# A half chunk of gate and up taken into the turns of the second seven-product chunk, in a one-core decoder layer

## The chip, the cores and the metric

The kernel runs on one core of a Trainium2 chip. The metric is the device time in microseconds (us) of one execution. Before the change the median of three runs is 292.05 us (291.76 to 292.76).

## The reference, cut to what matters

One decoder layer over 256 tokens with a model width of 1024. The first half (attention heads and a convolution side by side, then an output projection) is not touched by the change. The second half is a SwiGLU feed-forward network with a hidden width of 2816:

```python
h = rms_norm(x, norm2_g[l])
x = x + (jax.nn.silu(h @ w_gate[l]) * (h @ w_up[l])) @ w_down[l]
```

All values are float32. The kernel gets that precision out of TensorE by splitting each operand into a rounded high part and the rest, and by three matmuls for each product (high by high, high by low, low by high).

## The kernel before, in words

Tokens lie in two row blocks of 128 (i = 0, 1). The 2816 gate and up columns are cut into chunks (`WIDTHS`): chunks 0 to 2 and 4, 5 with 512 columns of each, chunk 3 with 256 (the half chunk). Two ways of computing a chunk stand side by side:

- A plain chunk is computed as it is written. Its units are `("g", c, z, kh, a)`, or `("h", 3, 0, kh, a)` for the half chunk, where gate and up share one weight block. Each unit has four products (L892 to L904). The half chunk has four units, here h0 to h3, and two PSUM banks, `fg30` and `fg31`.
- A shared chunk (1, 4 and 5) uses a seven-product scheme in place of eight: units s0 to s6 (`shared_unit`, L906 to L921), each with four products. Its weights are sums of blocks. s1 and s2 need an addition on VectorE (L271) for each of their two pieces; each of these additions is followed by an accumulating DMA (L285), issued by GpSimd, that makes the sum which s4 or s6 will use. The partial products go to the banks U and V (tag "s", two banks) and, at s3, W (tag "t", two banks).

The down-projection follows as row units f0 to f21 (`row`, L925), four products each: for both row blocks and both halves of the output, one tile of 128 hidden rows. Its four accumulators `pd` take the four banks of tag "mm" when f0 begins, in the order `pd00`, `pd01`, `pd10`, `pd11`; the half chunk's `fg30` and `fg31` are the last two tenants of that tag before them.

Weights come in blocks of 1 MB by DMA from SyncE's queue, in the order in which they are used: four buffers of tag "raw", and three homes (`big_h`, `big_l`, `side`) for the blocks of the shared chunks that are used more than once. Half a block is a piece of 1024 columns. `feed` (L265) turns pieces into operands: the addition where there is one (VectorE), the rounded copy `wh` (ScalarE, L272), and the difference `wl` (VectorE, L277). A plain unit or a row unit takes one piece, a shared unit takes two. `feed` is called when a unit begins, and once more in the middle of a shared unit. At piece number `at` it puts out additions and copies up to piece at + 5 and differences up to piece at + 4. Seven buffers hold split pieces, so the copy of a piece waits until TensorE has finished the piece seven before it.

The work after a product (silu, products with the gate, transposes back) is put out by tasks. `step` (L226) runs after every second product, that is in the middle and at the end of each unit. When h3 is done, `gate2_task` (L817, two silu on ScalarE) runs at the end of the next unit; `up2_task` (L821) puts out the first of two `times` (L813, VectorE, which read `fg30` and `fg31`) in the middle of the unit after that, the second at its end, and then the transposes (`turned`, L801 to L809), half a unit apart: TensorE into a bank of tag "t", then a ScalarE copy (L807) and a VectorE difference (L809).

Each engine keeps the order in which instructions were written (`keep_order`, L175). Buffers and banks are given out by the framework, which adds the waits. An engine may run far ahead of the others within these waits. The order of the units is what `_order` (L70) returns.

Of the kernel before, what the change touches and what calls it, by code (L numbers as in the profile page):

```python
# [64 lines left out]
SHARED = (1, 4, 5)  # L65
HOMES = ("big_h", "big_l", "side")
FIRST_TURN = 3


def _order():  # L70

    chunk = lambda c: [("g", c, z, kh, a) for z in range(2) for kh in range(2) for a in range(2)]
    rows = lambda a, b: [("f", f) for f in range(a, b)]
    order = [("g", 0, z, kh, a) for kh in range(2) for z in range(2) for a in range(2)]

    def stage(c, others):
        for j in range(8):
            if j < 7:
                order.append(("s", c, j))
            order.append(others[j])  # L80

    stage(1, chunk(2))
    order.extend(("h", 3, 0, kh, a) for kh in range(2) for a in range(2))
    stage(4, rows(0, 8))
    stage(5, rows(8, 16))
    return order + rows(16, NF)


def _plan():
# [15 lines left out]
    for kind, *unit in _order():  # L105
        if kind != "s":
            i, a = (base + unit[0] // 2, unit[0] % 2) if kind == "f" else (block[tuple(unit[:3])], unit[3])
            if a == 0:
                loads.append(i)
            sources.append((i, a, None, (("load",),) if a else ()))  # L110
            continue
        c, j = unit
        n = SHARED.index(c)
        b11, b21, b12, b22 = quarters[n]
        after = (None,) * 4 if n + 1 == len(SHARED) else quarters[n + 1]
        i, add, more, then = ((b11, None, None, None), (b11, b12, (b12, b22), None), (b11, b22, (b11, b21), None),
                              (b21, None, None, "load"), (b12, None, None, after[0]), (b22, None, None, after[2]),
                              (b11, None, None, after[3]))[j]
        if i == b21:
            loads.append(i)  # L120
        for a in range(2):
            acts = (("add",) + more,) if more else ()
            if a and then is not None:
                acts += (("load",),) if then == "load" else (("home", then),)
            sources.append((i, a, add, acts))
# [67 lines left out]
def _build(nc, tc, t, ctx):  # L193
# [627 lines left out]
    def up2_task(c, banks, width):  # L821
        ups = []
        for i in range(NT):
            ups.append(times(c, i, banks[i][:, W - width:] if width < W else banks[i], ffn["s", c][i], width))
            yield 1
        yield 0 if c else FIRST_TURN
        for i in range(NT):
# [105 lines left out]
    for kind, *unit in _order():  # L933
        feed(at + LEAD)
        if kind in "gh":
            plain_unit(*unit)
        elif kind == "s":
            shared_unit(*unit)
            at += 1
        elif unit[0] < NF - LAST:  # L940
            for i in range(NT):
                for n in range(2):
                    row(unit[0], i, n, wpart(at, n))
        else:
            last[unit[0]] = at
        at += 1
# [66 lines left out]
```

## Time and profile before

| what | value |
|---|---|
| median of three runs | 292.05 us |
| the profiled execution's own time | 291.87 us |
| its span, first to last instruction | 290.1 us |
| TensorE (PE) busy | 282.8 us, 97% |
| VectorE (DVE) busy | 226.3 us, 78% |
| ScalarE (ACT) busy | 181.8 us, 63% |
| GpSimd (POOL) busy | 24.9 us, 9% |
| HBM read | 61.55 MB |

The profile is of one execution. PE is TensorE's matmuls, PEld its weight loads, SPq the queue of SyncE that issues DMAs. A row of a timeline gives start, duration, engine, line of the kernel, operation, output and inputs by the program's names (buffer numbers left out) with their shapes, how many instructions were merged, and in brackets the idle time before it and who ended it. The durations of neighbours on PE overlap; the distance between two starts is what a matmul costs there.

### The profile page before, as it was taken

Reading aid. Unit: us, or ns where it says so; the run is one execution under the profiler, and the core shown is the slowest. Engines: PE = TensorE matmul, PEld = TensorE weight load, DVE = VectorE, ACT = ScalarE, POOL = GpSimd, SP = SyncE. Lnnn points to the kernel's source line nnn. Section 1 sums busy time; section 2 is a strip of 40 time slices with the busy share of each in tenths; the row PEclk is TensorE's granted clock in tenths of the full one; section 3 lists DMA queues with packets and bytes.
Section 4 is the critical chain, followed back from the end, with each engine's and each line's share of the span. In section 5 each row is a group of like instructions: output and inputs, shape, how many; then the busy total and the mean of one; then the engine's idle time right before and its main releaser. Section 6 shows DMA issues by size and latency. Waiting matters only on the chain.

```text
span 290.1 us, 3686 instructions
## 1 busy us (share of the span) xinstructions
PE 282.8 (97%) x1321; PEld 229.8 (79%) x1321; DVE 226.3 (78%) x339; ACT 181.8 (63%) x271; POOL 24.9 (9%) x46
## 2 busy tenths in 40 slices
PE   8999999999999999999999999889999999999994
PEld 6888877678688888888888888678888888888883
DVE  3899995999972957999997759978779996787211
ACT  5776768989815778655987453667754487656000
POOL 0005372000000000010200001120001020000000
PEclk9999999999999999999999999999999999999999
DMA  7999878643704589359999961897795888300011
GB/s 252 415 414 353 351 245 300 236 145 137 297 4 145 184 311 375 139 172 225 189 370 375 337 224 19 157 242 252 298 359 158 165 204 323 129 16 2 0 72 74
DMA packets 12052, 62.84 MB, mean 217 GB/s; under 512 B 1601, under 2 KB 2209, under 8 KB 6274
## 3 DMA queue, kind: packets, MB, share of 16 engines
q1 hardware_dynamic: 9874, 54.86, 50.6%
q0 software_dynamic: 2016, 7.74, 14.0%
q8 instruction: 10, 0.16, 0.2%
q14 instruction: 8, 0.07, 0.1%
q10 hardware_dynamic: 144, 0.00, 0.0%
HBM read 61.55 MB, written 1.05 MB: 216 GB/s over the span
## 4 chain that ended last, share of the span: by engine, by line
PE 92%; DVE 3%; DMA 1%; issue 1%; ACT 1%; SPq 0%; ACTq 0%
PE pd L723 20%; PE p L684 18%; PE fg L723 17%; PE U L723 10%; PE po L723 8%; PE V L723 6%; PE W L723 3%; PE aT L804 2%; DMA Y<-dw_b 1%; PE warm L341 1%; PE S L527 1%; DVE wl L277 1%; PE pT L557 1%; DVE raw L271 1%; PE x2T L746 1%
## 5 line engine op out<-in xcount | busy, mean ns | idle before, releaser
L277 DVE TENSOR_TENSOR wl<-raw,wh 128x1024 fp32r<-128x1024 f32 x108 | 129.5, 1221 | 11.4 <-ACT wh L272 10.9
L272 ACT ACTIVATE wh<-raw 128x1024 fp32r<-128x1024 f32 x108 | 111.8, 1057 | 35.6 <-DVE raw L271 12.5
L723 PE MATMUL pd<-wh,act 128*128 128x512 f32 x176 | 57.4, 393 | 1.8 <-DVE ac L813 1.8
L723 PE MATMUL fg<-wh,g 128*128 128x512 f32 x160 | 52.1, 394 | 0.0
L723 PEld LDWEIGHTS pd<-wh,act 128*128 128x128 f32 x176 | 33.1, 188 | 8.9 <-issue 2.2
L723 PEld LDWEIGHTS fg<-wh,g 128*128 128x128 f32 x160 | 30.1, 188 | 6.1
L723 PE MATMUL pd<-wl,act 128*128 128x512 f32 x88 | 34.3, 390 | 0.0
L684 PE MATMUL p<-wh,xh 128*128 128x512 f32 x80 | 33.0, 412 | 0.0
L684 PE MATMUL p<-wh,xl 128*128 128x512 f32 x80 | 31.4, 392 | 0.0
L723 PE MATMUL fg<-wl,g 128*128 128x512 f32 x80 | 31.2, 390 | 0.0
L684 PE MATMUL p<-wl,xh 128*128 128x512 f32 x80 | 26.6, 394 | 0.0
L285 POOL DMA_DIRECT2D raw<-w x12 | 10.5, 876 | 179.5 <-DVE raw L271 118.4
L807 ACT ACTIVATE act<-aT 128x512 fp32r<-128x512 f32 (+1 forms) x12 | 6.6, 560 | 21.4 <-PE aT L804 21.4
L723 PEld LDWEIGHTS pd<-wl,act 128*128 128x128 f32 x88 | 16.6, 188 | 3.3
L684 PEld LDWEIGHTS p<-wh,xh 128*128 128x128 f32 x80 | 15.2, 190 | 3.7 <-issue 0.7
L684 PEld LDWEIGHTS p<-wh,xl 128*128 128x128 f32 x80 | 15.2, 189 | 3.1
L684 PEld LDWEIGHTS p<-wl,xh 128*128 128x128 f32 x80 | 15.2, 189 | 3.0
L723 PEld LDWEIGHTS fg<-wl,g 128*128 128x128 f32 x80 | 15.1, 188 | 2.9
L809 DVE TENSOR_TENSOR act<-aT,act 128x512 fp32r<-128x512 f32 (+1 forms) x12 | 7.7, 645 | 11.8 <-ACT act L807 11.8
L723 PE MATMUL U<-wh,g 128*128 128x512 f32 x48 | 16.1, 392 | 0.0
L271 DVE TENSOR_TENSOR raw<-raw,raw 128x1024 f32<-128x1024 f32 x12 | 14.6, 1218 | 0.0
L723 PE MATMUL po<-wh,mixh 128*128 128x512 f32 x32 | 12.6, 395 | 0.0
(179 smaller groups left out, 413.8 us busy)
## 6 DMA issues: line engine op xcount, KB each, us to landing
raw<-w SPq DMA_DIRECT2D x45, 1024.0 KB, 5.1
raw<-w POOLq DMA_DIRECT2D x12, 512.0 KB, 5.5
first<-first SPq DMA_DIRECT2D x8, 384.0 KB, 5.8
xtok<-xtok SPq DMA_DIRECT2D x2, 512.0 KB, 9.1
x<-xtok SPq DMA_DIRECT2D x2, 512.0 KB, 7.4
out<-o SPq DMA_DIRECT2D x4, 256.0 KB, 2.0
inv<-inv POOLq DMA_DIRECT2D x1, 768.0 KB, 7.5
fwd<-fwd POOLq DMA_DIRECT2D x1, 648.0 KB, 4.3
```

What stands on the lines that cost most here:

```text
L271: nc.vector.tensor_tensor(src, src, blocks[add][:, cut(a)], op=ALU.add)
L272: nc.scalar.activation(dst[0], src, AF.Copy)
L277: nc.vector.tensor_tensor(dst[1], src, dst[0].bitcast(F32), op=ALU.subtract)
L285: nc.gpsimd.dma_start(blocks[to][:, cut(a)], t["w"][more - 2][:, cut(a)], accum_op=ALU.add)
L341: nc.tensor.matmul(warm[:, 0:T], zeros[:, 0:P], zeros, start=True, stop=True)
L527: nc.tensor.matmul(banks[a][:, out], G["qT"][rows, j, q], G["kT"][rows, j, k], start=True, stop=True)
L557: nc.tensor.transpose(b[:, a * P:(a + 1) * P], p[:, a * P:(a + 1) * P], ident)
L684: nc.tensor.matmul(banks[i], (xh, xh, xl)[a][:, kt, sls[i]], w[a % 2], start=kt == 0 and a == 0, stop=kt == KT - 1 and a == 2 - (order[-1] ...
L723: nc.tensor.matmul(bank, l, r, start=start and a == 0, stop=stop and a == 2, skip_group_check=on)
L804: nc.tensor.transpose(b[:, a, :], u[:, a * P:(a + 1) * P], ident)
L807: nc.scalar.activation(hi, b[:, 0:nf, :], AF.Copy)
L809: nc.vector.tensor_tensor(lo, b[:, 0:nf, :], hi.bitcast(F32), op=ALU.subtract)
```

## The change

Before, the four units of the half chunk stand alone, and then the units of chunk 4 take turns with f0 to f7. After, the half chunk's units are the first partners of chunk 4, and the row units begin after s3. The list `MIXED` fixes the turns ("s" is the next shared unit, "p" the next of the others):

- before: h0 h1 h2 h3 | s0 f0 s1 f1 s2 f2 s3 f3 s4 f4 s5 f5 s6 f6 f7
- after: h0 s0 h1 h2 s1 h3 s2 s3 f0 f1 s4 f2 f3 s5 f4 s6 f5 f6 f7

Counted from h0's piece as piece 0, the pieces before are h0 to h3: 0 to 3, s0: 4 and 5, f0: 6, s1: 7 and 8, f1: 9, s2: 10 and 11, f2: 12, s3: 13 and 14, f3: 15, s4: 16 and 17. After, they are h0: 0, s0: 1 and 2, h1: 3, h2: 4, s1: 5 and 6, h3: 7, s2: 8 and 9, s3: 10 and 11, f0: 12, f1: 13, s4: 14 and 15, f2: 16, f3: 17, s5: 18 and 19. Stages 1 and 5 keep their turns. The number of instructions of every kind stays the same. The list of loads follows the same order, so the block of s3 is now loaded ahead of the blocks of f0 to f3.

```diff
+MIXED = "psppspssppsppspsppp"
...
-    def stage(c, others):
-        for j in range(8):
-            if j < 7:
-                order.append(("s", c, j))
-            order.append(others[j])
-
-    stage(1, chunk(2))
-    order.extend(("h", 3, 0, kh, a) for kh in range(2) for a in range(2))
-    stage(4, rows(0, 8))
-    stage(5, rows(8, 16))
+    def stage(c, others, turns):
+        others = iter(others)
+        j = iter(range(7))
+        for turn in turns:
+            order.append(("s", c, next(j)) if turn == "s" else next(others))
+
+    half = [("h", 3, 0, kh, a) for kh in range(2) for a in range(2)]
+    stage(1, chunk(2), "spspspspspspspp")
+    stage(4, half + rows(0, 8), MIXED)
+    stage(5, rows(8, 16), "spspspspspspspp")
```

## The prediction

> **What bounds the kernel now.** I read the page's busy times first, then the waits of TensorE (PE), then a table of stages around the change, then the timelines of each engine there.
>
> ```profile
> PE 282.8 (97%) x1321; PEld 229.8 (79%) x1321; DVE 226.3 (78%) x339; ACT 181.8 (63%) x271; POOL 24.9 (9%) x46
> ```
>
> PE is busy nearly throughout, so a reordering that leaves every matmul in place can gain only where PE stands still. The waits of PE, by line, with total, count and longest in us:
>
> ```profile
> PE pd L723 <- DVE ac L813: 1.8, 1, 1.8
> PE warm L341 <- DVE one L324: 1.0, 1, 1.0
> PE cv L296 <- DVE yl L254: 0.2, 1, 0.2
> ```
>
> The second is at the start and the third in the convolution. In the feed-forward part there is one wait: an accumulator `pd` of the down-projection waits for `ac`, the product on VectorE (DVE) that reads the half chunk's banks. The table of stages (window, length, then busy time of PE, weight loads, DVE, ACT, POOL, granted clock, DMA share) puts it in its surroundings:
>
> ```profile
> 171.00:183.40 12.40, 12.40 (x63) 10.23 (x62) 9.26 (x11) 5.07 (x7) 1.75 (x2) 1.00 0.41 108
> 183.40:189.40 6.00, 4.24 (x19) 3.20 (x18) 6.00 (x7) 3.96 (x7) 0.23 (x1) 1.00 0.80 178
> 189.40:202.20 12.80, 12.78 (x58) 10.58 (x59) 10.23 (x11) 8.73 (x11) 1.52 (x2) 1.00 0.87 228
> ```
>
> The first row is h0 to h3: PE is full, DVE has about 3 of 12.4 us free. The second is s0 and f0: DVE is full, PE is not. The clock is 1.00 in all three, so the only price is the stall itself. PE's timeline:
>
> ```profile
> 186.12 0.39 PE L723 MATMUL pd<-wh,act 128*128 128x512 f32 x1
> ...
> 187.02 0.39 PE L723 MATMUL pd<-wl,act 128*128 128x512 f32 x1
> 187.25 0.39 PE L723 MATMUL pd<-wh,act 128*128 128x512 f32 x1
> 189.42 0.47 PE L723 MATMUL pd<-wh,act 128*128 128x512 f32 x1 [1.78 <-DVE ac L813]
> ```
>
> Six matmuls of f0 (two accumulators) run from 186.12; the seventh, `pd10`, needs the bank of `fg30`. Matmuls start 0.23 us apart (187.02 to 187.25), so it was due at 187.48 and began at 189.42: 1.94 us are lost. DVE's rows tell why:
>
> ```profile
> 169.17 1.22 DVE L277 TENSOR_TENSOR wl<-raw,wh 128x1024 fp32r<-128x1024 f32 x1
> 173.71 0.69 DVE L809 TENSOR_TENSOR act<-aT,act 128x512 fp32r<-128x512 f32 x1 [3.32 <-ACT act L807]
> 174.31 0.74 DVE L813 SCALAR_TENSOR_TENSOR ac<-fg,rstd,sf 128x512 f32<-128x512 f32 x1
> 174.97 1.22 DVE L277 TENSOR_TENSOR wl<-raw,wh 128x1024 fp32r<-128x1024 f32 x1
> 176.11 0.74 DVE L813 SCALAR_TENSOR_TENSOR ac<-fg,rstd,sf 128x512 f32<-128x512 f32 x1
> 176.77 1.22 DVE L271 TENSOR_TENSOR raw<-raw,raw 128x1024 f32<-128x1024 f32 x1
> 177.90 1.22 DVE L277 TENSOR_TENSOR wl<-raw,wh 128x1024 fp32r<-128x1024 f32 x1
> ...
> 186.53 1.22 DVE L271 TENSOR_TENSOR raw<-raw,raw 128x1024 f32<-128x1024 f32 x1
> 187.66 1.22 DVE L277 TENSOR_TENSOR wl<-raw,wh 128x1024 fp32r<-128x1024 f32 x1
> 188.79 0.87 DVE L813 SCALAR_TENSOR_TENSOR ac<-fg,rstd,sf 128x256 f32<-128x256 f32 x2
> ```
>
> The four L271 additions of s1 and s2 (the first at 176.77, the last at 186.53) stand in DVE's queue right before the two half-width `ac`. Starts of neighbours give what each operation costs in a full queue: 1.14 us for an addition or a difference, 0.66 for a full-width `ac`, 0.60 for an L809. ScalarE's (ACT) rows:
>
> ```profile
> 167.23 0.68 ACT L798 ACTIVATE sg<-U,rstd 128x512 f32<-128x512 f32 x1
> 167.80 2.00 ACT L272 ACTIVATE wh<-raw 128x1024 fp32r<-128x1024 f32 x2
> ...
> 186.55 0.82 ACT L798 ACTIVATE sf<-fg,rstd 128x256 f32<-128x256 f32 x2
> 188.82 0.58 ACT L858 ACTIVATE s<-U 128x512 f32<-128x512 f32 x1
> ```
>
> The two silu were done at 187.37, so `ac` lacked nothing but its turn on DVE. A copy L272 costs ACT 0.95 to 1.06 us.
>
> **The change, part by part.** PE executes the same matmuls. One unit costs it
>
> ```profile
> 196.97 2.72 PE U L723 x12
> ```
>
> 2.72 us, plus the transposes that fall into it.
>
> *Where PE stands.* The first five units are h0 to h3 and s0 before, h0, s0, h1, h2, s1 after, with the same transposes in them. So h3 now begins at 186.12, s2 at 188.84, s3 at 191.56, f0 at 194.28, and `pd10` is due at 195.64.
>
> *What DVE does until then.* The order in which it is written, from the additions on (piece numbers of the section on the change): addition 5 stands ahead of the difference that began at 169.17, and both end by 171.5 in DVE's free stretch before 173.71. Then: L809 173.71, `ac` 174.31, addition 6 at 174.97, difference 5 at 176.11, `ac` 177.25, difference 6 at 177.91, addition 8 at 179.05, difference 7 at 180.19, two L809 from 181.33, addition 9 at 182.53, difference 8 at 183.67. The copy of piece 9 waits for addition 9 (183.75) and ends at 184.8. From there copies and differences follow each other at 1.14: differences 9 to 14 begin at 184.9, 186.0, 187.2, 188.3, 189.5, 190.6. Then comes the first half-width `ac` at 191.8 (0.44 us, half of the 0.87), difference 15 at 192.2, and the second `ac` at 193.4.
>
> *Against what PE needs.* Piece 9 is used in the middle of s2, at 190.2, and is ready at 186.1; pieces 10 and 11 (s3, 191.56 and 192.92) are ready at 187.2 and 188.4. `pd10` is due at 195.64 and its bank is free at 192.4 (the earlier stall ended 0.2 after its `ac`); `pd11` about 0.7 later, its bank free at 194.0. Smallest cushion in this list: some 2 us at `pd11`. One more sits earlier: the transposes of chunk 2's second row block, in the middle of the unit after s0, at about 178.6, need the `ac` that now ends at 178.0, a cushion of 0.4 us. So the stall goes: minus 1.94 us.
>
> *What is late next.* s3 now has W in one of the two banks of tag "t" while the half chunk's transposes come in f0. Those rows, from the timelines of the three engines before:
>
> ```profile
> 192.23 0.38 PE L804 MATMUL aT<-c_ident,ac 128*128 128x128 f32 x2
> 192.64 0.38 ACT L807 ACTIVATE act<-aT 128x256 fp32r<-128x256 f32 x1 [2.29 <-PE aT L804]
> 193.06 0.42 DVE L809 TENSOR_TENSOR act<-aT,act 128x256 fp32r<-128x256 f32 x1 [1.13 <-ACT act L807]
> 193.84 0.38 PE L804 MATMUL aT<-c_ident,ac 128*128 128x128 f32 x2
> ```
>
> The second pair starts 1.61 after the first; the first bank is free 1.25 after it (193.48), and some 0.2 for the signal. Before, another bank was free anyway; now W has it, so the second pair must wait for the first pair's bank (margin 0.2 us), or for W's, which is read by the next DVE operation:
>
> ```profile
> 205.16 0.69 DVE L863 TENSOR_TENSOR c<-W,s 128x512 f32<-128x512 f32 x1 [0.40 <-PE W L723]
> ```
>
> Bounds: nothing, if the first bank is given and ACT and DVE are free then (my table has ACT's queue empty by 194.5 and DVE's by 194.9); 0.4 if it is W's (0.36 for the L809 ahead of it, 0.69 for itself, less the margin); with one late copy ahead of L807, up to 1.5. I take 0.05, because that table leaves both engines a us. A gain here is excluded: no wait stood there.
>
> *DMAs and queues.* s1 and s2 are moved ahead of f0 to f2, and with them their four accumulating DMAs on GpSimd's queue:
>
> ```profile
> 178.60 0.88 POOL L285 DMA_DIRECT2D raw<-w  x1 [38.11 <-ACT act L807]
> 182.22 0.87 POOL L285 DMA_DIRECT2D raw<-w  x1 [2.75 <-DVE raw L271]
> DMA to landing us min/median/max: 5.3/5.5/6.8
> ```
>
> Those of s1 now go out after additions 5 and 6, at about 171 and 176.5, and land by 183.3 at the latest; the copies that read them (pieces 14 and 15) come at 189 and 191: 6 us of cover. GpSimd has nothing else queued. The blocks that the additions read come from SyncE's queue:
>
> ```profile
> 151.35 1.46 SPq L245 DMA_DIRECT2D raw<-w  x2
> 156.32 3.60 SPq L245 DMA_DIRECT2D raw<-w  x2
> DMA to landing us min/median/max: 4.7/6.0/8.4
> ```
>
> The block for s1's additions is the first of the pair at 151.35, the one for s2's the first at 156.32: landed by 159.8 and 164.7, needed at 169.2 and 179.0. Nothing. The loads for f0 to f7 go out later in the turn order, but each goes four blocks ahead of its use, over 20 us; DMA was used at 0.41 in the first stage. U's last reader is the silu at 167.23, before s0's new start at about 174. Nothing.
>
> [...] The 182.22 row stood in a stretch where DVE never paused, and took 0.87 as its neighbour did. [...]
>
> *Sum.* 291.87 − 1.94 + 0.05 = 290.0 for an execution like the profiled one, which lies 0.18 below the median of the runs shown; 292.05 − 1.89 = 290.2 by the median. I forecast **290.0**.
>
> **The rivals.**
>
> 1. *The stall goes (forecast), 289.5 to 290.4.* For: the waiting `ac` gets three more units, 8.2 us, between h3 and f0's need, of which the moved additions' backlog takes none. Chance 0.66.
> 2. *A shorter wait takes its place, at the second transposes of the half chunk:* 0.4 to 1.5 as above, so 290.4 to 291.5. For: two banks, three tenants within one unit. Against: the margin is positive by the rows. Chance 0.14, nearly all under 291.2.
> 3. *Nothing is gained, 291.5 to 292.5.* The additions and the neighbours s2 s3 (four pieces in 5.4 us) could push DVE's queue out so that `ac` is late again; DVE's 1.14 for a piece against PE's 1.36 speaks against it, but additions, L809 and `ac` come on top, and my table would have to be wrong by 3 us. Chance 0.11.
> 4. *Slower: the second accumulating DMA of s1 lands late.* ACT takes its queue in order: the copy of piece 15 would hold back that of piece 16, the copy L858, that of piece 17 and the L807 of the transposes in f0, and the second transposes hold PE. That chain is 3 × 1.0 + 0.58 + 0.38 + 0.42 + 0.2, about 4.6 us, so it decides if the landing is after 192.7. [...] Against: 9 us of margin over the worst landing of the rows. Chance 0.05. [...]
>
> Other mishaps (the 0.4 us cushion at 178.6, a load in the wrong order) get 0.04, slower.
>
> **How the numbers follow.** The range 289.5 to 291.4 takes the first case and nearly all of the second: 0.8. About 0.3% (0.9 us) is what a measurement of this kernel can tell from no change. Faster by more than that, under 291.2: 0.66 + 0.12 = 0.78. Within it: 0.02 + 0.11 = 0.13. Slower: 0.05 + 0.04 = 0.09.
>
> **What would show it right or wrong.** Right: the wait of `pd` for `ac` is gone from PE's waits; the first L271 of the stage starts near 169 in place of 176.77 and the fourth near 182.5; the half-width `ac` run near 192 and 193.5, before f0; f0 starts near 194.3 without a pause inside. Case 2: a PE wait at `aT` for L809 or L863 within f0. Case 3: the wait of `pd` remains, with L277 rows ahead of `ac`. Case 4: ACT idle before an L272 with a DMA as what ended it. The forecast is wrong if PE's busy time shrinks by less than the span, that is if new waits add up to over 1 us.

## The result, and the profile after

The changed kernel takes 289.98 us in the median (289.64 to 290.64), the kernel before beside it 292.18: a ratio of 0.9926, with a 95% interval of 0.9901 to 0.9952. The profiled execution of the changed kernel took 289.81 us, its span is 288.0 us (before 291.87 and 290.1). The lines after are one higher than before from `_order` on (L271 is now L272, L813 is L814).

First the waits of PE after, in the columns of the prediction (line and what it waited for, total, count, longest):

```profile
PE warm L342 <- DVE one L325: 1.0, 1, 1.0
PE cv L297 <- DVE yl L255: 0.2, 1, 0.2
```

The wait of `pd` for `ac` is gone and no other has come. The stage table after, for the same two windows:

```profile
171.00:183.40 12.40, 12.40 (x63) 10.23 (x61) 10.22 (x12) 5.70 (x8) 1.75 (x2) 1.00 0.72 157
183.40:189.40 6.00, 6.00 (x28) 4.98 (x27) 5.95 (x6) 5.55 (x7) 1.75 (x2) 1.00 0.72 209
```

VectorE (the third busy time) does 10.22 us in the first window, 1.0 more than before. In the second it is still full, 5.95 of 6.00, but PE is full too: what stands in its queue then is no longer needed at once. VectorE's timeline after:

```profile
169.18 1.22 DVE L272 TENSOR_TENSOR raw<-raw,raw 128x1024 f32<-128x1024 f32 x1
170.31 1.22 DVE L278 TENSOR_TENSOR wl<-raw,wh 128x1024 fp32r<-128x1024 f32 x1
...
182.54 1.22 DVE L272 TENSOR_TENSOR raw<-raw,raw 128x1024 f32<-128x1024 f32 x1
183.67 8.17 DVE L278 TENSOR_TENSOR wl<-raw,wh 128x1024 fp32r<-128x1024 f32 x7
191.76 0.48 DVE L814 SCALAR_TENSOR_TENSOR ac<-fg,rstd,sf 128x256 f32<-128x256 f32 x1
192.15 1.22 DVE L278 TENSOR_TENSOR wl<-raw,wh 128x1024 fp32r<-128x1024 f32 x1
193.28 0.48 DVE L814 SCALAR_TENSOR_TENSOR ac<-fg,rstd,sf 128x256 f32<-128x256 f32 x1
193.68 1.22 DVE L278 TENSOR_TENSOR wl<-raw,wh 128x1024 fp32r<-128x1024 f32 x1
196.48 0.42 DVE L810 TENSOR_TENSOR act<-aT,act 128x256 fp32r<-128x256 f32 x1 [1.58 <-ACT act L808]
196.82 0.68 DVE L864 TENSOR_TENSOR c<-W,s 128x512 f32<-128x512 f32 x1
```

The first addition fills the idle time that stood before 173.71, and the fourth runs at 182.54 (before at 186.53). Seven differences follow, and then the two half-width `ac`, before f0. PE's timeline there:

```profile
194.28 0.39 PE L724 MATMUL pd<-wh,act 128*128 128x512 f32 x1
...
195.41 0.39 PE L724 MATMUL pd<-wh,act 128*128 128x512 f32 x1
195.64 0.38 PE L805 MATMUL aT<-c_ident,ac 128*128 128x128 f32 x2
195.78 0.48 PE L724 MATMUL pd<-wh,act 128*128 128x512 f32 x1
...
197.02 0.39 PE L724 MATMUL pd<-wh,act 128*128 128x512 f32 x1
197.25 0.38 PE L805 MATMUL aT<-c_ident,ac 128*128 128x128 f32 x2
```

f0 runs through. The transposes at 195.64, the first to need the first half-width `ac`, come 3.4 us after its end (191.76 + 0.48), the seventh matmul (195.78) 3.5. The second transposes start at 197.25, before the end of L864 (197.50), so they did not get W's bank but that of the first transposes, which L810 left at 196.90.

### The profile page after: what moved, and what is told of

Read it like the earlier page. It is cut to its first block, busy times and chain, and to the rows that moved or that the text cites. A ratio compares the mean times of both kernels' runs of the same rounds, so it can differ in the third digit from the quotient of the medians.

```text
span 288.0 us, 3690 instructions
## 1 busy us (share of the span) xinstructions
PE 282.5 (98%) x1321; PEld 229.5 (80%) x1321; DVE 225.9 (78%) x339; ACT 181.3 (63%) x271; POOL 24.9 (9%) x46
## 4 chain that ended last, share of the span: by engine, by line
PE 95%; DVE 3%; issue 1%
PE pd L724 21%; PE fg L724 19%; PE p L685 18%; PE U L724 11%; PE po L724 8%; PE V L724 6%; PE W L724 3%; PE aT L805 2%; PE warm L342 1%; PE S L528 1%; PE pT L558 1%; PE x2T L747 1%; PE cv L297 1%; DVE wl L278 0%; PE cv L298 0%
## 5 line engine op out<-in xcount | busy, mean ns | idle before, releaser
L810 DVE TENSOR_TENSOR act<-aT,act 128x512 fp32r<-128x512 f32 (+1 forms) x12 | 7.7, 646 | 12.9 <-ACT act L808 12.9
L272 DVE TENSOR_TENSOR raw<-raw,raw 128x1024 f32<-128x1024 f32 x12 | 14.6, 1218 | 0.0
```

Source lines behind the costliest of these rows:

```text
L272: nc.vector.tensor_tensor(src, src, blocks[add][:, cut(a)], op=ALU.add)
L810: nc.vector.tensor_tensor(lo, b[:, 0:nf, :], hi.bitcast(F32), op=ALU.subtract)
```

## The experiments

Ten kernels, each timed against the kernel before on the same chip. The theory: PE waited because the half-width `ac` stood in VectorE's queue behind the additions and differences when `pd10` was due; whatever moves `ac` ahead of that time removes the wait, in whole, and nothing else counts. The rivals: that the distance of f0 from h3 is what counts (B), that the additions must be gone before h3 ends (A). Line numbers shift by the lines that an edit adds, and the rows of one stage lie up to 0.6 us apart between the runs (the first accumulating DMA of s1 goes out at 171.01 in the change, at 170.75 in e8 and at 171.38 in e10).

| run | ratio to the kernel before (95%) | median, us | PE's waits in the stage |
|---|---|---|---|
| the change | 0.9926 (0.9901 to 0.9952) | 289.98 | none |
| e1_far_late | 0.9935 (0.9917 to 0.9953) | 290.23 | none |
| e2_near_early | 0.9914 (0.9898 to 0.9931) | 289.62 | none |
| e3_evict_first | 0.9925 (0.9910 to 0.9941) | 289.92 | none |
| e4_no_adds | 0.9929 (0.9911 to 0.9947) | 289.95 | none |
| e5_two_more | 0.9954 (0.9941 to 0.9966) | 290.44 | 0.4 |
| e6_four_more | 1.0034 (1.0022 to 1.0046) | 292.92 | 1.6 + 0.4 + 0.4 |
| e7_late_dma | 1.0284 (1.0269 to 1.0298) | 300.37 | 7.9 |
| e8_less_late | 1.0281 (1.0265 to 1.0296) | 300.29 | 7.9 |
| e9_dma_first_late | 1.0144 (1.0127 to 1.0161) | 296.03 | 4.5 |
| e10_dma_in_time | 0.9926 (0.9912 to 0.9939) | 289.93 | 0.3 |

**Distance without early additions.** On the kernel after (f1 and s2 change places as well as f0 and s1, as the order in brackets below says):

```diff
-MIXED = "psppspssppsppspsppp"
+MIXED = "ppppsspsppspspspspp"
```

> The kernel before with only the units s1 and f0 exchanged (h0 h1 h2 h3 s0 s1 f0 s2 f1 f2 s3, then as before): the four additions stay late in VectorE's queue (pieces 6, 7, 9 and 10 in place of 7, 8, 10 and 11), but f0 stands one unit further from h3. Theory (what counts is where the half-width ac stands in VectorE's queue against the time at which pd10 is due): the first ac starts near 188.9 and pd10 is due at 190.2, so the wait at pd10 goes and at most 0.3 us is left at pd11: 290.0 to 290.5. Rival A (the additions must be gone from the queue before h3 ends): the wait of some 1.9 us stays, 292.

The wait is gone, 290.23. VectorE's timeline of this run:

```profile
184.63 1.22 DVE L272 TENSOR_TENSOR raw<-raw,raw 128x1024 f32<-128x1024 f32 x1
185.76 2.52 DVE L278 TENSOR_TENSOR wl<-raw,wh 128x1024 fp32r<-128x1024 f32 x2
188.20 0.48 DVE L814 SCALAR_TENSOR_TENSOR ac<-fg,rstd,sf 128x256 f32<-128x256 f32 x1
```

and the seventh matmul of f0 on PE:

```profile
190.17 0.48 PE L724 MATMUL pd<-wh,act 128*128 128x512 f32 x1
```

The fourth addition begins at 184.63, 1.9 us earlier than before but after the end of h3 (183.4), and the first `ac` at 188.20, still too late for a `pd10` due at 187.48. It comes in time because `pd10` is now due one unit later. Rival A falls.

**Early additions without distance.** On the kernel after:

```diff
-MIXED = "psppspssppsppspsppp"
+MIXED = "pspspspsppsppspsppp"
```

> The kernel after with plain turns, h0 s0 h1 s1 h2 s2 h3 s3 f0: the additions are early (pieces 4, 5, 7 and 8), but only one unit stands between h3 and f0, as in the kernel before. Theory: no addition is left in VectorE's queue by then, the first ac starts near 193.8 (after silu near 192.7 to 193.5) and pd10 is due at 195.6: no wait, 290.0. Rival B (the distance of f0 from h3 is what counts, the additions are by the way): a wait of 1 to 2 us at pd10, 291 to 292.

The wait is gone, 289.62 (from the change's 289.98 the intervals don't separate it). VectorE, then PE:

```profile
193.13 1.23 DVE L278 TENSOR_TENSOR wl<-raw,wh 128x1024 fp32r<-128x1024 f32 x1 [1.01 <-ACT wh L273]
194.27 0.87 DVE L814 SCALAR_TENSOR_TENSOR ac<-fg,rstd,sf 128x256 f32<-128x256 f32 x2
```

```profile
195.24 0.39 PE L724 MATMUL pd<-wh,act 128*128 128x512 f32 x1
195.46 0.39 PE L724 MATMUL pd<-wl,act 128*128 128x512 f32 x1
195.69 0.62 PE L724 MATMUL pd<-wh,act 128*128 128x512 f32 x2
```

One unit between h3 and f0 is enough once no addition is in the queue: both `ac` are over at 195.14, and PE's stream of f0 has no gap (the last row holds the sixth and the seventh matmul). Rival B falls.

**No unit moved.** On the kernel before:

```diff
-            yield 1
+            yield (0, 3)[i] if c == 3 else 1
...
-                spawn(gate2_task(c, banks[0], T), EVICT)
-                spawn(up2_task(c, banks[0], T), EVICT + 1)
+                spawn(gate2_task(c, banks[0], T), 0)
+                spawn(up2_task(c, banks[0], T), 1)
```

> The kernel before with its order of units untouched; only the half chunk's two silu and two ac are put out one and two half units earlier (middle and end of s0), the two ac together, ahead of the fourth addition; the transposes stay where they were. Theory: the ac run at 186.5 and 186.9 in place of 188.8 and 189.2, pd10 (due 187.48) and pd11 (188.2) find their banks free, and PE doesn't wait: 290.0 to 290.2, all that the change brought without moving a unit. Rival B (order and distance of the units count): 292.

289.92, no wait. VectorE's timeline, then the two silu on ScalarE:

```profile
184.54 1.22 DVE L271 TENSOR_TENSOR raw<-raw,raw 128x1024 f32<-128x1024 f32 x1
...
186.81 0.87 DVE L813 SCALAR_TENSOR_TENSOR ac<-fg,rstd,sf 128x256 f32<-128x256 f32 x2
187.60 1.21 DVE L271 TENSOR_TENSOR raw<-raw,raw 128x1024 f32<-128x1024 f32 x1
```

```profile
184.22 0.82 ACT L798 ACTIVATE sf<-fg,rstd 128x256 f32<-128x256 f32 x2
```

The two `ac` stand ahead of the fourth addition, and their silu run 2.3 us earlier than before. With no unit moved, that gives all that the change gave.

**The additions left out.** On the kernel before, in `_plan`:

```diff
+        if c == 4:
+            add = None
```

> The kernel before without the four VectorE additions of chunk 4 (that part of the weight sums is left out; the accumulating DMAs stay). Theory: 4 x 1.14 us less in the queue ahead of ac, so ac runs before pd10 is due at 187.48: no wait, 290.0 to 290.2. Rival B: the wait stays nearly whole, as ac is put out only in the middle of f0: 291.5 to 292.

289.95, no wait; the `ac` run at 185.59:

```profile
184.45 1.23 DVE L279 TENSOR_TENSOR wl<-raw,wh 128x1024 fp32r<-128x1024 f32 x1 [0.49 <-ACT wh L274]
185.59 0.87 DVE L815 SCALAR_TENSOR_TENSOR ac<-fg,rstd,sf 128x256 f32<-128x256 f32 x2
```

So with order and distance as before, the additions' time is what made the wait, and rival B falls here too. Part of that time was spent on ScalarE: its copies wait for the additions (before, the one at 185.59 stood 1.55 us for one), and without them the silu run at 184.32 in place of 186.55.

**How much room the change left.** On the kernel after, with 2 or 4 repeats of one difference ahead of the first half-width `ac` (the lines for 2; for 4, `range(5 ...)`):

```diff
-            nc.vector.tensor_tensor(dst[1], src, dst[0].bitcast(F32), op=ALU.subtract)
+            for _ in range(3 if j == 72 else 1):
+                nc.vector.tensor_tensor(dst[1], src, dst[0].bitcast(F32), op=ALU.subtract)
```

> The kernel after with the difference of piece 14 done three times over (two more VectorE operations of 1.14 us, right ahead of the first half-width ac; nothing else changes). Theory (a queue with a measured cushion): the first ac starts near 194.0 in place of 191.76, pd10 (195.8) and pd11 (196.5) still find their banks free, but the L810 of the half chunk's first transposes moves to 197.1 to 197.5, so the second transposes, due at 197.25, wait some 0.4 us for their bank: 290.0 to 290.5, one PE wait of about 0.4 at aT. Rival C (VectorE's load in this stage counts as a whole, there is no cushion): plus 2.3, 292.3.

> The same with four more operations (4.5 us). Theory: the first ac ends near 196.8, PE waits 1.3 us for it at the transposes in the middle of f0 (due 195.64), then some 0.6 us at pd11 for the second ac and 0.8 us at the second transposes: 2.7 us in all, 292.7. Rival C: plus 4.5, 294.5. Rival D (PE's queue takes the pause up elsewhere): under 291.

Both came out as the theory had them: 290.44 and 292.92, that is 0.5 and 2.9 above the change's median (expected up to 0.5 and 2.7); by the ratios in the table it is 0.8 and 3.2, and the change's own interval is some 0.7 us wide to either side. PE's timeline with two repeats, then with four:

```profile
197.80 0.44 PE L806 MATMUL aT<-c_ident,ac 128*128 128x128 f32 x2 [0.39 <-DVE act L811]
```

```profile
197.78 0.41 PE L806 MATMUL aT<-c_ident,ac 128*128 128x128 f32 x2 [1.62 <-DVE ac L815]
...
199.31 0.47 PE L725 MATMUL pd<-wh,act 128*128 128x512 f32 x1 [0.42 <-DVE ac L815]
...
200.68 0.44 PE L806 MATMUL aT<-c_ident,ac 128*128 128x128 f32 x2 [0.44 <-DVE act L811]
```

2.3 us more on VectorE made 0.4 us of waits on PE, 4.5 us made 2.5, so rivals C and D fall: the queue has room, and beyond it the delay comes through. With four, the first wait is at the first transposes, which stand just ahead of `pd10` and read the first `ac`. The tightest place after the change is the second transposes, as in the prediction's second case: it takes little to bring that wait out.

**A late accumulating DMA.** This makes the prediction's slower case happen. On the kernel after, the DMA of piece 6 is held on GpSimd's queue behind a one-column operation that reads the difference of piece 12 (`j == 70`) or 10 (`j == 68`):

```diff
+            if j == 70:
+                nc.gpsimd.tensor_tensor(seen, dst[1][:, 0:1].bitcast(F32), one, op=ALU.mult)
+                nc.gpsimd.dma_start(*held.pop(), accum_op=ALU.add)
...
+                    if j == 64:
+                        held.append((blocks[to][:, cut(a)], t["w"][more - 2][:, cut(a)]))
+                        continue
```

> The kernel after with the second accumulating DMA of s1 (piece 6) held back on GpSimd's queue behind a one-column operation that reads the difference of piece 12 (ends near 189.6), so it goes out near 189.9 in place of 176.5 and lands near 195.4. Theory (the prediction's fourth case: ScalarE's and VectorE's queues pass the delay on): the copy of piece 15 waits until 195.4, the difference of piece 15 and the second half-width ac stand behind it (ac ends near 198.1, pd11 waits some 1.8 us), and the transposes' copy and difference end near 199.7 (some 0.8 us more at the second transposes): plus 2.6, 292.6. Rival E (piece 15 itself is due only at 201, so its late arrival is covered): 290.0.

> The same with the DMA held behind the difference of piece 10 (ends near 187.3): out near 187.6, landing near 193.1. Theory: pd11 still finds its bank free (ac ends near 195.8, due 196.45), the L810 of the first transposes ends near 197.5 and the second transposes wait some 0.4 us: 290.4; the point from which the delay decides lies between 192 and 193. Rival E: 290.0 and no wait of PE.

Both came out slower, as e7 was expected to, but far beyond the 292.6 and 290.4: PE stood 7.9 us in both. The DMA went out at 190.98 and 188.17 (e8's rows lie 0.5 us earlier throughout, so 2.3 us apart in the schedule), and landed 11.0 and 13.2 us after its issue. ACT, then PE, then the stage table (the last four columns: granted clock, DMA share, GB/s) of e7_late_dma:

```profile
202.05 2.00 ACT L273 ACTIVATE wh<-raw 128x1024 fp32r<-128x1024 f32 x2 [10.90 <-DMA raw<-w]
```

```profile
204.90 0.76 PE L732 MATMUL pd<-wh,act 128*128 128x512 f32 x1 [7.90 <-DVE ac L822]
```

```profile
190.00:196.90 6.90, 6.90 (x32) 5.43 (x30) 2.51 (x3) 1.15 (x3) 1.86 (x2) 1.00 1.04 268
...
204.90:208.30 3.40, 3.40 (x9) 2.54 (x10) 3.38 (x5) 2.15 (x5) 0.00 (x0) 0.50 0.75 284
208.30:210.00 1.70, 1.70 (x5) 1.31 (x5) 1.24 (x2) 1.59 (x3) 0.00 (x0) 0.50 0.58 135
```

The 300.37 lies 10.4 us above the change's median, 2.5 beyond the wait. The clock of 0.50 accounts for that: from the end of the pause to about 210 matmuls start 0.43 us apart (205.46 and 205.89) in place of 0.23 (194.33 and 194.56), and 5.1 us at about half the pace lose some 2.5. Rival E (piece 15 is not due before 201) falls: PE stood from 197.0, some 4 us before piece 15 was due, because the copy of piece 15 held back the whole of ACT's queue (idle for 10.90 us before it), its difference VectorE's (idle for 10.62), and so the second `ac` and `pd11`. VectorE's work does not explain the late landing: it stood idle from 192.5 to 203.1 in e7, and so through 9.4 of the DMA's 11.0 us.

Two more runs put the late DMA ahead of the two of s2 in GpSimd's queue, to find the point from which it decides (`if j in (64, 66, 67)` is held until `j == 68`; `(64, 66)` until `j == 67`):

> As the run with the DMA held behind the difference of piece 10, but the two accumulating DMAs of s2 are held with it and go out after it, so that it has GpSimd's queue to itself: out near 188.2, landing 5.5 to 6.8 us later, 193.7 to 195. Theory: the landing decides from about 192.9 (the chain from the copy of piece 15 to the second transposes of the half chunk, 4.3 us, against 197.25), and each us after that is a us of PE's wait, which shows first at pd11: a wait of 0.8 to 2.1 us, 290.8 to 292.1, clock 1.00 throughout. If the two runs before were late because of the DMA engines' load and not because two accumulating DMAs stood ahead in the queue, it lands at 199 or later again and PE waits over 5 us.

> The same, held behind the difference of piece 9 (ends near 186.1): out near 187.2 after the one-column operation, landing near 192.7. Theory: no wait or one of at most 0.3 us, 290.0 to 290.3. With an accumulating DMA that lands late for the load of the DMA engines: over 293.

e10_dma_in_time came as expected, e9_dma_first_late did not: first in the queue, issued at 188.47, the DMA still took 9.8 us, where the one issued at 187.68 in e10 took 6.0. That is nearer to what was expected for the load of the DMA engines (landing at 199, over 5 us) than for the place in the queue (193.7 to 195), so a place in the queue is not enough to explain the late landings. ACT and PE of e9, then of e10:

```profile
198.39 2.00 ACT L273 ACTIVATE wh<-raw 128x1024 fp32r<-128x1024 f32 x2 [7.47 <-DMA raw<-w]
```

```profile
201.25 0.77 PE L733 MATMUL pd<-wh,act 128*128 128x512 f32 x1 [4.48 <-DVE ac L823]
```

```profile
193.81 2.01 ACT L273 ACTIVATE wh<-raw 128x1024 fp32r<-128x1024 f32 x2 [2.57 <-DMA raw<-w]
```

```profile
198.05 0.44 PE L814 MATMUL aT<-c_ident,ac 128*128 128x128 f32 x2 [0.26 <-DVE act L819]
```

Against the landing, though, the chain is what was expected: a copy that starts at 193.81 costs 0.3 us of wait at the second transposes, one at 198.39 costs 4.5 us at `pd11`. Less their waits the copies give 193.5 for the transposes (193.1 in the times of the change, as e10's rows lie 0.4 later) and 193.9 for `pd11`; the expectation had 192.9 for the transposes.

## Why the prediction was right

*The term of the sum.* Minus 1.94 us for the stall. The rows at the start of the stage agree to 0.01 us in the two traces (the transposes at 165.15 before, 165.16 after), and the last addition of the output starts at 286.00 before and 283.97 after: 2.03 us, the stall and some 0.1 for PE's restart (its first two matmuls start 0.31 apart in place of 0.23). The sum gave 290.0, the median is 289.98. That they lie 0.02 apart is luck: the sum was made from the profiled execution, and the medians measured side by side differ by 2.20 where the sum had 1.89. The 0.05 taken for the second transposes was not needed.

*VectorE's queue, written out by hand.* The list set the fourth addition at 182.53, the two `ac` at 191.8 and 193.4, f0 at 194.28; the trace has 182.54, 191.76, 193.28 and 194.28. What made this work is that starts of neighbours (1.14 us) were added up and not durations (1.22), and that the engines' own orders were followed through the waits, such as the copy of piece 9 behind addition 9. Two small readings were off without harm: the first transposes of the half chunk, which come ahead of `pd10` and put it at 195.78 in place of 195.64, and the cushion at 178.6, which was 0.8 us and not 0.4 (the transposes stayed at 178.84, the `ac` was over at 177.99).

*The cause.* e3 and e4 show it with the units in their old order: the wait goes when `ac` is moved ahead of one addition, and when the additions are left out. In both the silu come over 2 us earlier too, so they do not separate VectorE's queue from ScalarE's. An estimate from the rows before (first silu over near 187.0, 0.48 for `ac`, 0.2 for the signal, `pd10` due at 187.48) leaves some 0.2 us of wait with the silu in their old place and VectorE free, so nearly all of the wait was VectorE's queue. e1 and e2 show that the change does two things, more distance and earlier additions, and that each of them alone is enough here. The change brings both, which is its room of 3.4 us.

*The second case* (a wait at the second transposes). It did not come, by a margin of about 0.3 us; e5 and e10 show that this is the next place to give, at 0.4 and 0.3 us. The wait in e5 ended with L811 (the first transposes' difference) and not with W's reader, so the bank given was that of the first transposes, the lower bound of the prediction. The prediction's 0.4 us for W's bank does not come out of the terms named beside it (0.36 + 0.69 less 0.2 is 0.85), but it fits the rows after: L864 ends at 197.50, 0.25 after the second transposes were due, and 0.2 for the signal make 0.45.

*The third case* (no gain) asked for the hand-written list to be wrong by 3 us; it was within about 0.1. One sign of being wrong was put the wrong way round: when a wait goes, PE's busy time need not shrink with the span. It went from 282.8 to 282.5 while the span fell by 2.1. What the sign was meant to catch, new waits of over 1 us, did not come.

*The fourth case* did not come either: the DMA went out at 176.49 and landed 5.6 us later, over 8 us before its use. What a late landing does is real (e7 to e9, where the issue was held back); that it comes late by itself was not seen in the change. The prediction's chain lacked a link: the late wait shows first at `pd11`, through VectorE's difference of piece 15. The expectations of e7 and e8 had 5.5 us from issue to landing, where the held DMAs took 6.0 (e10) to 13.2 (e8), and their price left out the clock of 0.50. GpSimd's rows after, and the landing of the second:

```profile
171.01 0.88 POOL L286 DMA_DIRECT2D raw<-w  x1 [30.50 <-DVE raw L272]
176.49 0.88 POOL L286 DMA_DIRECT2D raw<-w  x1 [4.60 <-DVE raw L272]
```

```profile
DMA to landing us min/median/max: 5.6/5.6/5.6
```

VectorE ran without a pause from 173.71 to 194.9, mostly with additions and differences. The DMA issued at 176.49 landed in that stretch, and its 5.6 us lie within the 5.3 to 6.8 of the kernel before.

## What to carry to other kernels

When PE waits for a short operation on another engine, look at what stands in front of that operation in its engine's queue, and at when the waiting bank is due: both are read from starts in the trace, and a list of queue times made from them forecast the new schedule to 0.1 us. Moving the short operation ahead of long ones that nobody needs yet can bring as much as a new order of the work. After such a change, the smallest remaining cushion (here 0.3 us at a shared PSUM bank) is worth knowing, because the next edit that adds to the queue will meet it first.

## What the runs showed of the hardware that was not expected

The accumulating DMAs of 512 KB that GpSimd issues landed 5.3 to 5.6 us after their issue when they were 2.6 us or more apart, 6.1 to 6.8 when 1.6 to 1.9 apart, all in the kernel before. In the changed kernel the second of s2 goes out 1.0 us after the first and takes this long, covered there:

```profile
186.46 0.88 POOL L286 DMA_DIRECT2D raw<-w  x1 [0.17 <-issue]
```

```profile
DMA to landing us min/median/max: 10.0/10.0/10.0
```

Beside it, blocks of 1 MB from SyncE's queue (issued at 188.47 and 190.74) took 8.1 and 8.2 us. The DMA share was about 1.0 from 191 us on in the changed kernel and in e9. In e9, with a block issued 0.03 us after it, the first in the queue took 9.8. e2 has the same without any queue: its first accumulating DMA of s1, 29 us after the one before it, has a block of SyncE issued 0.5 us behind it (169.68), which took 8.7 us itself:

```profile
169.14 0.87 POOL L286 DMA_DIRECT2D raw<-w  x1 [28.38 <-DVE raw L272]
```

```profile
DMA to landing us min/median/max: 9.1/9.1/9.1
```

So an accumulating DMA can be late with none ahead of it in the queue. That the block right behind it is the reason, and what the queue adds, stays open.

PE's granted clock stayed at 1.00 over the pauses of 1.8 us (before) and 0.3 us (e10), and was 0.50 after 4.5 us (e9) and 7.9 us (e7). The stage table of e9:

```profile
197.00:200.00 3.00, 0.00 (x0) 0.00 (x0) 0.52 (x1) 1.61 (x2) 0.00 (x0) 1.00 1.09 296
200.00:203.00 3.00, 1.75 (x6) 1.22 (x6) 3.00 (x5) 2.09 (x4) 0.00 (x0) 0.53 1.00 178
203.00:207.00 4.00, 4.00 (x12) 3.13 (x11) 3.60 (x5) 2.88 (x4) 0.00 (x0) 0.50 1.01 372
```

In the last row matmuls start 0.43 us apart (203.53 and 203.96), where it was 0.23 before the pause (194.32 and 194.55). No pause between 1.8 and 4.5 us was measured, so the length from which the clock falls stays open. In these runs a wait cost about its own length only where it was short: the 1.94 us of the kernel before cost 2.03 by the last additions, while against the change's median 7.9 us of waiting cost 10.4, and 4.5 us cost 6.1.
